# Issuing the stores of the residual rows from ScalarE's queue instead of SyncE's in a hybrid RG-LRU, attention and routed-experts layer

## The chip, the cores and the metric

The kernel runs on one core of a Trainium2 chip. The metric is the time of one execution on the device, in microseconds (us). The time of the kernel before is the median of three runs. The rows further down come from one more execution, taken by the hardware profiler. Engines are named as the profile names them: PE (TensorE, matmuls), PEld (its weight loads), DVE (VectorE), ACT (ScalarE), POOL (GpSimd), and SPq (the queue of SyncE, which here does nothing but issue DMAs).

## The reference, cut to what matters

One layer works on 512 rows of 1024 numbers, all in float32. A mixer (a gated linear recurrence and differential attention) gives `mix`. Then:

```
x1 = x + m2 * (mix @ w_out)                      # the residual rows; 512 x 1024
h2 = rmsnorm(x1, g2) * (1 + m4) + m3
aff = softmax(h2 @ w_router)                     # 16 experts
g, idx = top_k(aff.T, 64)                        # every expert takes its 64 best rows
y_e = (silu(h2[idx] @ w_gate[e]) * (h2[idx] @ w_up[e])) @ w_down[e]
out = x1;  out[idx] += m5 * g * y_e              # for all 16 experts
```

Each expert has three matrices of 1024 by 2816, so the 16 experts read 554 MB. That is most of the bytes that the kernel moves.

## The kernel before

**Stages.** The rows are worked on in four tiles of 128 rows, t = 0 to 3. After the mixer, `out_proj(t)` loads the tile of x into `X1[t]`, multiplies by `w_out` on PE in two halves of 512 columns, scales each half by `m2` on DVE (L1051), adds it into `X1[t]` (L1052), and takes its sum of squares on ACT (L1053, an `activation` with `Square`). When both halves are done, `X1[t]` is stored to `out` (L1054, the line that the change touches). Tiles 0 and 1 are done in `early_proj` while the second half of the attention still runs, tiles 2 and 3 in `late_proj`. `route(t)` (L1115) transposes `X1[t]` on PE, copies the transposes to SBUF (`h2T`), multiplies by the router's weights (`pl`), and makes the softmax (`lg`, `aux`). `largest` (L1143) finds the 64 largest values of each expert on DVE by eight rounds of MAX8 and MATCH_REPLACE8. The result is `least` (L1170), the threshold of each expert. From it follow the slots `slT`, the one-hot matrices `oh`, and with them `gather` (L1248), which makes an expert's 64 rows `xe` on PE. Then the expert loop begins: `up_rows` (L1278) multiplies `xe` by `w_gate` and `w_up`, in eight steps k of 128 rows; `down_part` does the rest, and adds the result into `out` in memory by an indirect DMA from POOL (L1319).

**The ring.** The weights of the experts go through a ring of 14 slots of 1408 KB. The order of the slots is: two of `ring0` (in the profile `ring<-`; for k = 0 of expert 0 they are loaded long before the stage looked at here), four of `R2` (`r<-`), four of `ring1` (`ring<-`), four of `R3` (`r<-`), and round again. A load into a slot waits until what used this memory before is done: the `ring1` slots hold parts of `w_out` until the last `out_proj` has read them, and the last two `R3` slots lie where the router's small tiles are until `least` is there. All of these loads are issued from SP's queue, and so are the four stores of `X1[t]`. A queue is worked off in order: a DMA that waits holds up those behind it.

**The order of the instructions.** Up to the expert loop, instructions aren't issued as written. The class `Flow` records them and lists them at each `flush` with a cost model of its own: `cost` (L206) gives the time for which an instruction holds its engine, the time to its result, and the bytes of a DMA; `schedule` (L290) takes again and again the instruction with the earliest start, on one engine the one with the higher level `lvl` where several are ready. The level is the length of the longest chain that hangs on an instruction, plus a random part (`SEEDS`). Copies and additions made by `copy` and `tt` may go to either of two engines, whichever is done earlier. An entry for SP is taken in the order of recording (`i`). The flushes are at L620, L1076 (it ends with `early_proj(0)` and `early_proj(1)`), L1172 (`late_proj`, `route`, `largest`) and L1328 (slots, the loads of expert 0, the first one-hot). In the profile everything recorded in this way stands under line L288. The tile framework merges the flushes, so that on SP loads of the last flush stand between stores of the flush before it.

Of the kernel before, what the change touches and what calls it, by code (L numbers as in the profile page):

```python
# [56 lines left out]
class Flow:  # L57
# [93 lines left out]
    def tt(self, o, a, b, op):  # L151

        self.add("vec", "tensor_tensor", (o, a, b), {"op": op}, [("gp", "tensor_tensor", (o, a, b), {"op": op})])
# [52 lines left out]
    def cost(self, e, m, a, k, out, r):  # L206

        n = 1
        for st, c in out.ap[1:]:
            n *= c  # L210
        nin = n
        if r:
            nin = 1
            for st, c in r[0].ap[1:]:
                nin *= c
        ps = any("PSUM" in str(v.tensor.space) for v in r + [out] if type(v.tensor).__name__ == "Tile")
        if e == "sp":
            return 0.06, 0.06, 4 * n * out.ap[0][1], None
        if e == "pe":
            f32r = "float32r" in str(r[0].dtype)  # L220
            if m == "transpose":
                c = 0.084 if f32r else 0.109
            elif f32r:
                c = max(n * (1 if n >= 256 else 4), 256) * 0.00046
            else:
                c = 2 * max(0.112, n * 0.00084) * (0.5 if out.ap[0][1] < 128 else 1.0)
            return c, c + 0.165, 0.0, None
        ptr = sum(1 for v in r[1:] if not [1 for st, c in v.ap[1:] if c > 1])
        if e == "act":
            fn = a[2].name if hasattr(a[2], "name") else str(a[2]).split(".")[-1]  # L230
            c = (nin / 1120.0 + 0.14 if ps else nin / 1215.0 + 0.205) + 0.08 * ptr
            acc = 0.18 if "accum_out" in k else 0.0
            return c + (acc if acc else -0.1), c + acc, 0.0, self.SETS.get(fn)
        if e == "vec":
            if m == "memset":
                c = n / 1000.0 + 0.06
            elif m in ("max", "match_replace"):
                c = max(n, nin) / 960.0 + 0.14
            elif m in ("tensor_copy", "tensor_scalar") and not ps:
                c = n / 1920.0 + 0.15  # L240
            elif m == "tensor_tensor_scan":
                c = n * 2.1 / 960.0 + 0.14
            else:
                c = nin / 960.0 + 0.15
            c += 0.06 * ptr
            return max(c - 0.085, 0.06), c, 0.0, None
        if m == "tensor_tensor" and k.get("op") == OP.pow:
            c = 0.38 + 0.175 * n
        else:
            c = {"tensor_tensor": 2.5, "memset": 0.9, "iota": 1.5, "tensor_scalar": 1.2, "tensor_copy": 1.2}.get(m, 3.5) * n / 1000.0 + 0.18  # L250
        return max(c - 0.035, 0.06), c, 0.0, None
# [38 lines left out]
    def schedule(self, ops):  # L290
# [10 lines left out]
        while len(order) < len(ops):  # L301
# [23 lines left out]
            for e2 in o["alt"]:  # L325
                ready[e2].remove(o)
            cost, lat = o["alt"][e][3:]
            if e == "pe":
                w = int(st / WINDOW)
                if st > 15 and work.get(w - 1, 0.0) < 0.6 * WINDOW:  # L330
                    cost, lat = 2 * cost, lat + cost
                work[w] = work.get(w, 0.0) + min(cost, (w + 1) * WINDOW - st)
                if st + cost > (w + 1) * WINDOW:
                    work[w + 1] = work.get(w + 1, 0.0) + st + cost - (w + 1) * WINDOW
# [28 lines left out]
def hybrid_block_kernel(ctx: ExitStack, tc: tile.TileContext, x, cx, w_ada, b_ada, w_in, w_out, w_router, w_gate,  # L363
# [3 lines left out]
    act, vec, gp, pe, sp = (flow.proxy(e) for e in ("act", "vec", "gp", "pe", "sp"))  # L367
# [62 lines left out]
    def raw():  # L430
        return X.tile([128, D], F32, name="raw", tag="raw", bufs=4)
# [70 lines left out]
    def mm3(o, lh, ll, rh, rl, first, last):  # L502
        pe.matmul(o, lh, rh, start=first, stop=False, skip_group_check=True)
        pe.matmul(o, lh, rl, start=False, stop=False, skip_group_check=True)
        pe.matmul(o, ll, rh, start=False, stop=last, skip_group_check=True)
# [46 lines left out]
    def rstd(o, ssum, n, w):  # L552
        gp.tensor_scalar(ssum, ssum, 1.0 / n, EPS, op0=OP.mult, op1=OP.add)
        gp.tensor_tensor(o, ssum, half[:, :w], op=OP.pow)
# [471 lines left out]
    X1 = [raw() for _ in range(4)]  # L1026
# [15 lines left out]
    def out_proj(t, mh, ml, m2row, bank, tmp):  # L1042
        ts = slice(t * 128, (t + 1) * 128)
        sp.dma_start(X1[t], x[ts, :])
        for q in range(2):
            c2 = slice(q * 512, (q + 1) * 512)
            po = bank()
            for k in range(KT):
                mm3(po, mh[k], ml[k], woH[k][:, c2], woL[k][:, c2], k == 0, k == KT - 1)
            tm = tmp()  # L1050
            vec.tensor_tensor(tm, po, m2row[:, c2], op=OP.mult)  # L1051
            tt(X1[t][:, c2], X1[t][:, c2], tm, OP.add)  # L1052
            act.activation(tm, X1[t][:, c2], AF.Square, accum_out=s2[:, t, q:q + 1])  # L1053
        sp.dma_start(out[ts, :], X1[t])  # L1054
        vec.tensor_tensor(s2[:, t, 2:3], s2[:, t, 0:1], s2[:, t, 1:2], op=OP.add)
        rstd(rs2[:, t:t + 1], s2[:, t, 2:3], D, 1)

    def early_proj(t):
        h6, l6 = (LR.tile([128, 6, 128], F32R, name=f"g{i}", tag=f"g{i}", bufs=2) for i in range(2))
        hl2 = LR.tile([128, 2, 2, 128], F32R, name="xc", tag="xc", bufs=2)  # L1060
        mh, ml = mix_parts(t, ((6, h6, l6), (2, hl2[:, 0], hl2[:, 1])))
        out_proj(t, mh, ml, m2e, ac, lambda: QK.tile([128, 512], F32, name="hl", tag="hl", bufs=2))
# [47 lines left out]
    def late_proj(t):  # L1110
        mh, ml = parts2 if t == 2 else mix_parts(t, ((KT, *(RT.tile([128, KT, 128], F32R, name=n) for n in ("mh", "ml"))),))
        out_proj(t, mh, ml, m2l, po_bank,
                 lambda: RT.tile([128, 512], F32, name="tm", tag="tm", bufs=2))
# [215 lines left out]
    act, vec, gp, pe, sp = nc.scalar, nc.vector, nc.gpsimd, nc.tensor, nc.sync  # L1329
# [77 lines left out]
```

## Time and profile before

| | us |
|---|---|
| median of three runs | 1722.05 (1720.24 to 1722.1) |
| the profiled execution: its time | 1720.25 |
| the profiled execution: span of the trace | 1718.4 |

| engine | busy us | share of the span |
|---|---|---|
| PE | 1466.9 | 85% |
| PEld | 800.5 | 47% |
| DVE | 406.3 | 24% |
| ACT | 317.4 | 18% |
| POOL | 164.7 | 10% |

The DMA engines moved 607.32 MB, 353 GB/s over the span. The stage with the stores lies between 354 us and 404 us of the span, the expert loop from 424 us on. A time of the span is 1.85 us short of the execution's own time, which is around it.

### The profile page before, as it was taken

Reading aid. Unit: us, or ns where it says so; the run is one execution under the profiler, and the core shown is the slowest. Engines: PE = TensorE matmul, PEld = TensorE weight load, DVE = VectorE, ACT = ScalarE, POOL = GpSimd, SP = SyncE. Lnnn points to the kernel's source line nnn. Section 1 sums busy time; section 2 is a strip of 40 time slices with the busy share of each in tenths; the row PEclk is TensorE's granted clock in tenths of the full one; section 3 lists DMA queues with packets and bytes.
Section 4 is the critical chain, followed back from the end, with each engine's and each line's share of the span. In section 5 each row is a group of like instructions: output and inputs, shape, how many; then the busy total and the mean of one; then the engine's idle time right before and its main releaser. Section 6 shows DMA issues by size and latency. Waiting matters only on the chain. (4 is left out here: it accounts for less than half of the span.)

```text
span 1718.4 us, 19014 instructions
## 1 busy us (share of the span) xinstructions
PE 1466.9 (85%) x8072; PEld 800.5 (47%) x8072; DVE 406.3 (24%) x786; ACT 317.4 (18%) x565; POOL 164.7 (10%) x160
## 2 busy tenths in 40 slices
PE   6988989897998997888788878887987798779877
PEld 3786788675445442433253334433432443244323
DVE  5889986835010010001010001000000000000101
ACT  5466765421101010101010001101010101010101
POOL 1194172300000000000000000000000000000000
PEclk9989999897989999899989998999999899989999
DMA  9535321356999999999999999999999999999996
GB/s 343 155 107 166 109 72 64 106 198 282 403 412 428 421 427 422 428 420 421 429 427 422 421 428 423 426 421 429 420 429 421 428 421 429 421 427 421 429 422 259
DMA packets 89375, 607.32 MB, mean 353 GB/s; under 512 B 12393, under 2 KB 31046, under 8 KB 40266
## 3 DMA queue, kind: packets, MB, share of 16 engines
q1 hardware_dynamic: 86986, 601.91, 84.9%
q0 software_dynamic: 2304, 4.20, 1.4%
q8 instruction: 63, 1.03, 0.2%
q14 instruction: 22, 0.18, 0.0%
HBM read 599.78 MB, written 6.29 MB: 353 GB/s over the span
## 5 line engine op out<-in xcount | busy, mean ns | idle before, releaser
L1283 PE MATMUL gu<-r,xe 128*64 128x512 f32 (+1 forms) x1752 | 386.2, 564 | 66.1 <-DMA r<-in_w_up_dram 65.7
L1283 PE MATMUL gu<-ring,xe 128*64 128x512 f32 (+1 forms) x1320 | 302.4, 574 | 54.0 <-DMA ring<-in_w_up_dram 54.0
L1283 PEld LDWEIGHTS gu<-r,xe 128*64 128x64 f32 x1752 | 148.3, 138 | 286.1 <-issue 190.5
L1283 PEld LDWEIGHTS gu<-ring,xe 128*64 128x64 f32 x1320 | 111.7, 140 | 227.2 <-issue 150.3
L1307 PE MATMUL y<-r,hT 128*64 128x512 f32 (+1 forms) x888 | 206.6, 604 | 0.0
L1307 PE MATMUL y<-ring,hT 128*64 128x512 f32 (+1 forms) x648 | 151.2, 597 | 0.0
L1319 POOL DMA_INDIRECT out_dram<-ys,ix x16 | 25.0, 1564 | 1283.3 <-DVE ys L1318 1283.3
L1292 DVE TENSOR_TENSOR sg<-sg,gu 64x512 f32<-64x512 f32 x96 | 58.1, 647 | 326.4 <-ACT sg L1291 326.1
L1307 PEld LDWEIGHTS y<-r,hT 128*64 128x64 f32 x888 | 76.9, 148 | 107.8 <-issue 96.5
L1291 ACT ACTIVATE sg<-gu 64x512 f32<-64x512 f32 x96 | 48.1, 552 | 425.0 <-PE gu L1283 424.8
L288 PE MATMUL ac<-w,ring 128*128 128x256 f32 x768 | 108.5, 298 | 10.1 <-DVE ring L288 4.9
L1318 DVE SCALAR_TENSOR_TENSOR ys<-y,gate,brow 128x512 f32<-128x512 f32 x16 | 12.0, 751 | 407.9 <-issue 382.7
L288 PEld LDWEIGHTS ac<-w,ring 128*128 128x128 f32 x768 | 101.3, 201 | 13.5 <-issue 4.4
L1254 ACT ACTIVATE xe<-y,B,A 128x128 f32<-128x128 f32 x32 | 14.6, 457 | 502.1 <-PE y L1252 502.1
L1298 PE MATMUL tr<-ident,sg 64*128 64x64 f32 x352 | 57.9, 319 | 53.5 <-DVE sg L1292 42.2
L1268 DVE COPY gate<-tr 128x1 f32<-128x1 f32 x16 | 2.5, 158 | 392.4 <-PE tr L1264 392.4
L1307 PEld LDWEIGHTS y<-ring,hT 128*64 128x64 f32 x648 | 56.3, 146 | 76.9 <-issue 68.9
L1298 PEld LDWEIGHTS tr<-ident,sg 64*128 64x128 f32 x352 | 50.5, 232 | 73.3 <-issue 45.2
L1299 ACT ACTIVATE hT<-tr 128x512 f32<-128x512 f32 (+1 forms) x48 | 26.9, 561 | 223.4 <-PE tr L1298 192.9
L288 PE MATMUL ac<-ring,w 128*128 128x512 f32 (+1 forms) x240 | 62.7, 388 | 1.5 <-POOL w L288 1.2
L288 PEld LDWEIGHTS ac<-ring,w 128*128 128x128 f32 x240 | 40.7, 191 | 9.2 <-POOL w L288 1.3
L288 ACT ACT_TABLE_LOAD x33 | 42.3, 1283 | 4.9 <-DVE lru L288 3.6
(254 smaller groups left out, 1269.9 us busy)
## 6 DMA issues: line engine op xcount, KB each, us to landing
r<-in_w_gate_dram SPq DMA_DIRECT2D x73, 1408.0 KB, 26.9
r<-in_w_up_dram SPq DMA_DIRECT2D x73, 1408.0 KB, 27.0
r<-in_w_down_dram SPq DMA_DIRECT2D x73, 1408.0 KB, 26.9
ring<-in_w_gate_dram SPq DMA_DIRECT2D x55, 1408.0 KB, 26.8
ring<-in_w_up_dram SPq DMA_DIRECT2D x55, 1408.0 KB, 26.8
ring<-in_w_down_dram SPq DMA_DIRECT2D x54, 1408.0 KB, 26.8
raw<-in_w_ada_dram SPq DMA_DIRECT2D x32, 512.0 KB, 3.8
raw<-in_w_in_dram SPq DMA_DIRECT2D x20, 512.0 KB, 4.6
```

What stands on the lines that cost most here:

```text
L288: getattr(self.eng[e], o["m"])(*o["a"], **o["k"])
L1254: act.activation(xe[:, k], pg, AF.Identity, bias=B2[:, k:k + 1], scale=A2[:, k:k + 1])
L1268: vec.tensor_copy(g_t, pi[:, 2 * pair + i:2 * pair + i + 1])
L1283: pe.matmul(b[hh * 64:(hh + 1) * 64, :n], xe[:, k, es], wgu[k][hh][:, f:f + n], start=(k == 0), stop=(k == KT - 1), skip_group_check=True)
L1291: act.activation(sg[64:128, f:f + n], b[:64, :n], AF.Silu)
L1292: vec.tensor_tensor(sg[64:128, f:f + n], sg[64:128, f:f + n], b[64:128, :n], op=OP.mult)
L1298: pe.transpose(pt[:, j - j0], cols[:, j], ident[64:128, 64:128])
L1299: act.activation(hT[:, j0:j1], pt[:, :j1 - j0], AF.Copy)
L1307: pe.matmul(y[hh * 64:(hh + 1) * 64, a % 512:a % 512 + b - a], hT[:, j], wd[a // FE][:, a % FE:a % FE + b - a], start=(j == 0), stop=(j == ...
L1318: vec.scalar_tensor_tensor(ys, y, g_t, m5row, op0=OP.mult, op1=OP.mult)
L1319: gp.indirect_dma_start(out=out.rearrange("t (h d) -> (t h) d", h=2), out_offset=bass.IndirectOffsetOnAxis(ap=ix[:, :1], axis=0), in_=ys, ...
```

## The change

The store of `X1[t]` at L1054 is issued from ScalarE's queue. Since `act` entries had no cost for a DMA in the planner, `cost` gets one: such an entry holds ACT for 0.4 us, its result is there after 4.0 us, and no bytes are booked. (For SP the planner books 0.06 us and the bytes.)

```diff
@@ cost @@
         ptr = sum(1 for v in r[1:] if not [1 for st, c in v.ap[1:] if c > 1])
+        if m == "dma_start":
+            return 0.4, 4.0, 0.0, None
         if e == "act":
@@ out_proj @@
             act.activation(tm, X1[t][:, c2], AF.Square, accum_out=s2[:, t, q:q + 1])
-        sp.dma_start(out[ts, :], X1[t])
+        act.dma_start(out[ts, :], X1[t])
         vec.tensor_tensor(s2[:, t, 2:3], s2[:, t, 0:1], s2[:, t, 1:2], op=OP.add)
```

## Rows read from the trace of the kernel before

**Rows 1.** Busy time by stretch: start and end, length, engines, PE clock, DMA share, GB/s.

```profile
core 0: us, PE busy (x) PEld busy (x) DVE busy (x) ACT busy (x) POOL busy (x), PEclk, DMA share, GB/s
427.00:430.00 3.00, 3.00 (x17) 1.05 (x14) 0.00 (x0) 0.00 (x0) 0.00 (x0) 1.00 0.00 0
...
440.00:460.00 20.00, 20.00 (x111) 8.68 (x108) 0.00 (x0) 1.37 (x3) 0.00 (x0) 1.00 1.00 422
...
520.00:1590.00 1070.00, 915.71 (x4758) 419.58 (x4754) 71.97 (x167) 86.28 (x173) 20.15 (x13) 0.95 1.01 424
```

**Rows 2.** Waits from 520 to 1590 us: total, times, longest.

```profile
PEld gu L1283 <- DMA r<-in_w_up_dram: 71.6, 36, 3.6
```

**Rows 3.** Timeline of SP's queue, 365 to 430 us: start, duration, what.

```profile
365.85 0.34 SPq L288 DMA_DIRECT2D out_dram<-raw  x1
...
368.10 0.42 SPq L288 DMA_DIRECT2D r<-in_w_gate_dram  x1
380.49 0.34 SPq L288 DMA_DIRECT2D out_dram<-raw  x1
380.88 0.43 SPq L288 DMA_DIRECT2D r<-in_w_up_dram  x1
...
403.18 0.34 SPq L288 DMA_DIRECT2D out_dram<-raw  x1
403.62 0.38 SPq L288 DMA_DIRECT2D ring<-in_w_gate_dram  x1
...
415.36 0.33 SPq L288 DMA_DIRECT2D r<-in_w_gate_dram  x1
...
429.89 0.33 SPq L288 DMA_DIRECT2D ring<-in_w_gate_dram  x1
```

**Rows 4.** Waits of SP's queue from 350 to 460 us.

```profile
SPq L288 <- DVE raw L288: 33.0, 3, 11.9
SPq L288 <- PE po L288: 13.0, 1, 13.0
```

**Rows 5.** Timeline of all engines, 367 to 430 us; in brackets idle before, releaser.

```profile
367.18 7.74 PE L288 MATMUL po<-ring,w 128*128 128x512 f32 x32 [0.61 <-ACT m2row L288]
...
402.49 0.67 DVE L288 TENSOR_TENSOR raw<-raw,tm 128x512 f32<-128x512 f32 x1
...
406.90 0.21 DVE L288 SCALAR_TENSOR_TENSOR lg<-pl,rs,brt 128x16 f32<-128x16 f32 x1
...
409.27 0.28 DVE L288 COPY vals<-pT 16x128 f32<-16x128 f32 x1
...
414.99 0.21 DVE L288 TENSOR_REDUCE least<-tops 16x1 f32<-16x65 f32 x1
...
424.16 5.70 PE L1283 MATMUL gu<-ring,xe 128*64 128x512 f32 x24
```

**Rows 6.** Timeline of ACT, 364 to 408 us.

```profile
364.58 0.63 ACT L288 ACTIVATE hl<-raw 128x512 f32<-128x512 f32 x1 [9.39 <-issue]
...
366.55 0.58 ACT L288 ACTIVATE m2row<-po 128x512 f32<-128x512 f32 x1
...
382.61 0.60 ACT L288 ACTIVATE h2T<-pt 128x512 f32<-128x512 f32 x1 [1.23 <-PE pl L288]
...
404.21 0.60 ACT L288 ACTIVATE h2T<-pt 128x512 f32<-128x512 f32 x1 [0.29 <-PE pt L288]
407.49 0.31 ACT L288 ACTIVATE aux<-lg,s 128x16 f32<-128x16 f32 x1 [2.68 <-DVE s L288]
```

**Rows 7.** The four stores: duration in ns, min/median/max.

```profile
L288 SPq DMA_DIRECT2D out_dram<-raw x4: 344/344/348, 354.4 to 403.2; - x4
```

**Rows 8.** DMA issues of the whole run: count, KB, median us to landing.

```profile
r<-in_w_gate_dram SPq DMA_DIRECT2D x73, 1408.0 KB, 26.9
```

**Rows 9.** Loads into R2 and R3, 366 to 420 us, to landing.

```profile
DMA to landing us min/median/max: 7.5/11.4/15.2
```

**Rows 10.** Timeline of DVE, the same kind of copy as ACT's h2T.

```profile
385.44 0.69 DVE L288 COPY h2T<-pt 128x512 f32<-128x512 f32 x1 [1.45 <-PE pl L288]
```

## The prediction

> **What bounds the kernel now.** I read the stretches first, to see which resource is full where; then the waits in the expert loop; then SP's own timeline and waits around the stores; last the timeline of all engines between the last store and the first expert, to see what lets the loop begin.
>
> From 520 to 1590 us the DMA engines are full: share 1.01 at 424 GB/s, while PE is busy for 915.71 of 1070 us [rows 1], and PE's weight loads wait for arriving weights (71.6 us on one of the kinds of load) [rows 2]. So the loop is bound by the stream of weights, and the end of the kernel is the time at which this stream becomes continuous, plus its bytes at 424 GB/s. A change ahead of the loop counts only if it moves that time.
>
> When does the stream become continuous? SP issues the load for the first ring slot that comes free again at 429.89 us [rows 3]. Ahead of it, from 427 to 430 us, the DMA engines are empty: share 0.00 [rows 1]. Everything that the 14 slots can hold has landed by 427 us, and nothing more may be asked for until PE is through with step k = 0 of expert 0, which runs from 424.16 us for 5.70 us, to 429.86 us [rows 5]. That release, and not an arrival, starts the stream. Right after it, from 440 to 460 us, PE is busy for 20.00 of 20 us [rows 1]: the slots in hand are enough, and it waits for no load.
>
> What sets 424.16 us is the router. The second half of `X1[3]` is added from 402.49 us; its logits come at 406.90, the transposed affinities at 409.27, `least` at 414.99, then the slots, the one-hots, the first gather [rows 5]. This chain contains no load and no store.
>
> **The change, part by part.** *Taken from SP.* Four issues of 0.344 us [rows 7], 1.4 us, and the time for which SP stood at them: three waits on `X1` (DVE raw), 33.0 us in total, the longest 11.9 us [rows 4]. Two of them hold ring loads. The store of tile 2 stands from 368.10 + 0.42 us to 380.49 us before a load into R2 that goes at 380.88; the store of tile 3 at 403.18 us stands before a load into `ring1` that goes at 403.62 [rows 3]. Without the stores, the first of these loads can go some 12 us earlier. The second can go earlier too, but not before the load ahead of it, which is held for 13.0 us by PE's last reading of `w_out` (PE po) [rows 4], so until 380.88 + 13.0 = 394 us: it gains less than 403.6 − 394 = 9.6 us. The load issued at 415.36 us [rows 3] waits for `least`, which ends at 414.99 + 0.21 = 415.20 us [rows 5]; it doesn't move by this.
>
> What is late next? Nothing that these loads feed. They land before 427 us already, and earlier landing lengthens the empty stretch before 429.89 us by as much. Gain at the end: 0 us, hidden by the router's chain. If that cover were gone, and the expert loop began as its weights came, the gain would be up to 9.6 us.
>
> The Trainium skill has a rule that speaks against such a change: in "DMA: Bandwidth & Descriptors", section "Issuing engines are not separate DMA queues", it says that DMAs started from several engines share the same 16 DMA engines, and that this "will only save the time on the sequencer". By that the saving would be 4 × 0.344 = 1.4 us of SP's time; the trace shows that SP is also freed of 33.0 us of waiting, which the rule doesn't speak of. By the rule or by the rows, the sum at the end stays 0.
>
> *Added to ACT.* The trace shows no DMA issued from ACT. From below its cost is nothing, if the issue runs beside ACT's datapath; a gain by the issue itself is excluded, since ACT has one more thing to do. From above, the nearest row is SP's issue of the same transfer, 0.344 us [rows 7]. In the planner the store has no instruction behind it, so its level is about 4 (14 with the boost of the early tiles), below the Square and below the copies, on which the router's chain hangs. It will stand behind the second Square of its tile, which waits for the same addition; the store then adds no wait of its own on `X1`. Behind it on ACT stand:
>
> Tile 0: the Squares of tile 1, before which ACT is idle for 9.39 us [rows 6]; hidden, cost 0. Tile 1: the copy of `m2row` at 366.55 us [rows 6], for which PE waits to begin the matmuls of tile 2 at 367.18 us [rows 5]; here 0 to 0.34 us are on the path. Tile 2: copies to `h2T` at 382.61 us after 1.23 us of idle time [rows 6]; hidden. Tile 3: the second `h2T` copy of the last tile at 404.21 us, after only 0.29 us of idle time, and it is in the router's chain: 0.344 − 0.29 = 0.05 us; or, if the copy goes first, the idle 2.68 us before 407.49 us take it [rows 6]: 0. If all this cover failed, four issues would cost 1.4 us. The sum on the path lies between 0 and 0.4 us. I take 0.3 us, near the upper end, because the only row for such an issue is SP's and the copy of `m2row` follows without a gap.
>
> *Moved in the planner.* The entry of 0.4 us shifts ACT's free time in its model, and the bytes of the four stores are no longer booked. Levels of other instructions keep their values: the store's own cost in the level was 4.02 (0.06 + 2.5 + 1.46 for its bytes) and is 4.0, and longer chains than the store's hang on the additions. So the order changes only where ACT's or SP's free time decides. The likeliest such change is a copy that goes to the other of its two engines. An `h2T` copy on DVE takes 0.69 us [rows 10] where ACT takes 0.60 [rows 6], and DVE is the fuller engine in the router's chain; one more there costs at most 0.7 us, one fewer gains as much. I take 0 and keep −0.7 to +2.8 us (four copies, two of tile 2 and two of tile 3) for the range.
>
> Sum against the profiled execution: 1720.25 + 0.3 = 1720.6 us. That execution lies 1.8 us (0.1%) below the median of the runs shown, so on the median I say 1722.05 + 0.3, about 1722.3 us.
>
> **The rivals.** *A: the freed loads shorten the kernel.* SP loses 33.0 us of waiting [rows 4], and the loop is bound by loads. If the stream's beginning depended on SP, the gain would be the smaller of the two advances that I could bound, up to 9.6 us: 1722.05 − 9.6 = 1712.5 us. For it: the full DMA engines from 520 us on. Against it: share 0.00 just before 429.89 us, with all slots filled [rows 1]. This rival is in the Trainium skill as well: "Perfetto Trace Analysis", section "DMA Optimizations", advises one issuing engine for inputs and another for outputs, for more dynamic spread. No row here shows the advice at work; the rows show where its gain would be lost. Chance 0.04.
>
> *B: ACT stands at a store for a DMA ahead of it.* In the stream a load of 1408 KB takes 1.44 MB / 424 GB/s = 3.4 us and lands 26.9 us after its issue [rows 8, 1], so eight are under way; I read that as a limit of eight, with the next DMA held until the eighth before it has landed. If that limit counts over both queues, the store of tile 3 could find the loads that now run ahead of it unlanded. Loads of this stage take up to 15.2 us to land [rows 9]; one issued at 403.62 us would free ACT at 418.8 us, and the copy at 404.21 would come 14.6 us late: 1722.05 + 14.6 = 1736.7 us. It decides from the point at which eight ring loads stand between that store and the store of tile 2. Against it: between them there can be only one load into R2, four into `ring1` and two into R3, seven, because the next ones wait for `least`; the eighth back is then a DMA of about 380 us, long landed. Chance 0.05.
>
> *C: the planner's order changes for the worse* by more than copies: a matmul block of a late tile put behind a route, or a larger part of the router's chain behind `largest`. The rows bound it only loosely; four copies and the issue come to 2.8 + 0.4 = 3.2 us, 1725.3 us, and more than that needs a second misfortune. Chance 0.05 of more than 3.4 us slower; 0.02 that the new order gains as much.
>
> *D: the change doesn't do what it says*, because the loads freed on SP wait for memory anyway. Then the profile differs only by the stores' queue, and the time is the forecast's.
>
> **How the numbers follow.** A measurement of this kernel can tell about 0.2%, 3.4 us. The forecast, D included, has 0.84 and lies within that. Faster: A 0.04 and C 0.02, 0.06. Slower: B 0.05 and C 0.05, 0.10. The range takes the forecast's own bounds, which hold more than 8 in 10: the lowest run less one copy, 1720.24 − 0.7 = 1719.5 us; the highest run with four copies and the issue, 1722.1 + 2.8 + 0.4 = 1725.3 us.
>
> **What would show it.** In the profile after: stores under ACT's queue; the R2 load now at 380.88 us issued near 369; a `ring1` load issued between 394 and 403 us; the DMA engines empty for longer before the load that follows step k = 0; and that load within 1 us of 429.89. The forecast is wrong if that load moves by more than 3.4 us, or if ACT shows idle time before an `h2T` copy that a DMA ends.

## The result, and the profile after

| | before | after |
|---|---|---|
| median, us | 1721.42 (4 runs, 1720.24 to 1722.1) | 1740.22 (4 runs, 1738.95 to 1742.37) |
| span of the profiled execution, us | 1718.4 | 1739.5 |

The kernel became slower: ratio 1.0112 (95% interval 1.0100 to 1.0124), about 19 us. The forecast was no change.

SP's timeline of the kernel after (start, duration, what) answers to [rows 3]:

```profile
369.76 0.47 SPq L290 DMA_DIRECT2D r<-in_w_up_dram  x1
404.25 0.33 SPq L290 DMA_DIRECT2D r<-in_w_gate_dram  x1
...
418.99 0.33 SPq L290 DMA_DIRECT2D r<-in_w_gate_dram  x1
...
433.91 0.33 SPq L290 DMA_DIRECT2D ring<-in_w_gate_dram  x1
...
439.87 6.77 SPq L290 DMA_DIRECT2D r<-in_w_down_dram  x4
446.69 0.44 SPq L290 DMA_DIRECT2D ring<-in_w_gate_dram  x1
447.18 0.43 SPq L290 DMA_DIRECT2D ring<-in_w_up_dram  x1
447.66 0.44 SPq L290 DMA_DIRECT2D ring<-in_w_gate_dram  x1
448.15 0.47 SPq L290 DMA_DIRECT2D ring<-in_w_up_dram  x1
470.65 7.18 SPq L290 DMA_DIRECT2D ring<-in_w_down_dram  x4
```

The stores are gone, and the last load into `R2` goes at 369.76 instead of 380.88 us. But the four loads into `ring1` (k = 3 and 4 of expert 0), which before went from 394 to 404 us, now go from 446.69 us. They stand behind four loads of `w_down` into `R2`, and those wait for PE to be through with steps k = 1 and 2. Before, the same `w_down` loads came behind all of expert 0's other loads, as two more rows of SP's timeline before show:

```profile
394.11 0.33 SPq L288 DMA_DIRECT2D ring<-in_w_gate_dram  x1
...
435.85 6.77 SPq L288 DMA_DIRECT2D r<-in_w_down_dram  x4
```

A queue is worked off in order, so four slots stayed empty for 44 to 53 us longer than before.

PE's timeline of the kernel after (in brackets the idle time before, and what ended it):

```profile
445.74 1.16 PE L1254 MATMUL y<-oh,raw 128*128 128x128 f32 x8
461.30 1.94 PE L1285 MATMUL gu<-ring,xe 128*64 128x512 f32 x2 [14.40 <-DMA ring<-in_w_gate_dram]
464.53 6.50 PE L1285 MATMUL gu<-ring,xe 128*64 128x512 f32 x22 [1.29 <-DMA ring<-in_w_up_dram]
```

PE is ready for step k = 3 at 446.9 us and stands 14.40 + 1.29 = 15.7 us for weights. Busy time by stretch of the kernel after (the first, second and last row answer to [rows 1]; those between show PE's stand and the stretch behind it):

```profile
core 0: us, PE busy (x) PEld busy (x) DVE busy (x) ACT busy (x) POOL busy (x), PEclk, DMA share, GB/s
...
430.00:434.00 4.00, 4.00 (x21) 1.31 (x18) 0.00 (x0) 0.00 (x0) 0.00 (x0) 0.98 0.00 0
...
440.00:460.00 20.00, 6.90 (x40) 3.35 (x39) 0.00 (x0) 0.92 (x2) 0.00 (x0) 0.77 1.00 412
...
452.00:460.00 8.00, 0.00 (x0) 0.00 (x0) 0.00 (x0) 0.00 (x0) 0.00 (x0) 0.50 1.01 429
...
468.00:472.00 4.00, 4.00 (x24) 1.81 (x19) 0.00 (x0) 0.00 (x0) 0.00 (x0) 1.00 0.66 228
...
460.00:520.00 60.00, 52.28 (x276) 22.47 (x278) 4.04 (x10) 7.23 (x13) 0.00 (x0) 0.88 0.95 391
...
520.00:1590.00 1070.00, 922.78 (x4770) 422.53 (x4768) 74.67 (x176) 86.35 (x173) 21.93 (x14) 0.94 1.01 424
```

The stream is as fast as before (424 GB/s). It still becomes continuous at the load behind k = 0, now at 433.91 us, with the DMA engines empty ahead of it. What differs is how much had landed by then: 10 slots instead of 14, as these two rows of the 66 us ahead of that load show, first of the kernel before, then of the kernel after:

```profile
363.89:429.89 66.00, 53.17 (x271) 41.00 (x269) 34.70 (x131) 12.70 (x32) 2.71 (x9) 0.82 0.74 295
```

```profile
367.91:433.91 66.00, 53.07 (x256) 41.76 (x255) 33.19 (x128) 9.93 (x26) 3.04 (x10) 0.77 0.52 199
```

(295 − 199) GB/s × 66 us = 6.3 MB less; four loads are 5.77 MB, which take 13.6 us at 424 GB/s. (The rest is a load of x, 0.5 MB, which falls into the first of the two windows only.)

ACT is innocent. Its timeline in the kernel after, around two of the stores (answers to [rows 6]):

```profile
367.10 0.63 ACT L290 ACTIVATE hl<-raw 128x512 f32<-128x512 f32 x1 [0.61 <-DVE raw L290]
367.15 0.34 ACTq L290 DMA_DIRECT2D out_dram<-raw  x1
...
367.73 0.58 ACT L290 ACTIVATE m2row<-po 128x512 f32<-128x512 f32 x1
...
406.55 0.63 ACT L290 ACTIVATE tm<-raw 128x512 f32<-128x512 f32 x1 [0.45 <-DVE raw L290]
406.56 0.34 ACTq L290 DMA_DIRECT2D out_dram<-raw  x1
```

These two stores, and that of tile 2 at 382.17 us, are issued inside a Square, and the copy of `m2row` follows its Square without a gap. The store of tile 0 goes at 355.68 us, between the two Squares of its tile, and there too ACT has no idle time behind it.

**Where the order comes from.** The section on the kernel says that SP's entries are taken in the order of recording. This holds only among those that can start at once. Two lines of `schedule`, as they stand for SP (the terms for the other engines are left out at `...`):

```
st = rt[i] if rt[i] > f else f        # f: SP's clock; rt: when the slot is free
key = (st if st > f + 0.05 else f, i if e == "sp" else ...)
```

An entry whose slot comes free later than SP's clock is sorted by that time. This is the kernel's own list at its last flush, in the list's own times (a model's, not the chip's):

```
loads of expert 0      before (SP clock 366.66)    after (SP clock 312.14)
R2     k = 1, 2        366.66 to 366.84            312.14 to 312.32
ring1  k = 3, 4        366.90 to 367.08            357.49 to 362.73
R3     k = 5, 6        behind ring1                312.38 to 312.56
ring0  k = 7           367.38                      312.62 to 312.68
R2     w_down          374.66 to 386.68            320.14 to 332.15
ring1  w_down          behind R2's                 from 376.21
```

The store of tile 3 had put SP's clock at 366.66, later than the last release of a `ring1` slot that the list knows (358.19 to 363.6). All loads could then start at once, and recording order held. Without the stores SP's clock is 312.14. The `ring1` loads are then late, and are sorted behind every load whose release the list doesn't know. For `R3` it doesn't know the router's tiles, and for `ring0` and the second round of `R2` not PE's steps. It puts that second round, the `w_down` loads, 4.0 us apart at 320 to 332, where on the chip they wait until 439.87 us.

### The profile page after: what moved, and what is told of

It reads as the page before. It is cut to its first block, busy times and chain, and to the rows that moved or that the text cites. A ratio compares the mean times of both kernels' runs of the same rounds, so it can differ in the third digit from the quotient of the medians.

```text
span 1739.5 us, 19002 instructions
## 1 busy us (share of the span) xinstructions
PE 1477.2 (85%) x8072; PEld 805.0 (46%) x8072; DVE 408.5 (23%) x787; ACT 316.1 (18%) x563; POOL 165.4 (10%) x161
## 5 line engine op out<-in xcount | busy, mean ns | idle before, releaser
L1285 PE MATMUL gu<-r,xe 128*64 128x512 f32 (+1 forms) x1752 | 390.4, 570 | 64.9 <-DMA r<-in_w_up_dram 64.7
L1256 ACT ACTIVATE xe<-y,B,A 128x128 f32<-128x128 f32 x32 | 14.6, 458 | 496.1 <-PE y L1254 496.1
```

The lines of the kernel that those rows point to most:

```text
L1256: act.activation(xe[:, k], pg, AF.Identity, bias=B2[:, k:k + 1], scale=A2[:, k:k + 1])
L1285: pe.matmul(b[hh * 64:(hh + 1) * 64, :n], xe[:, k, es], wgu[k][hh][:, f:f + n], start=(k == 0), stop=(k == KT - 1), skip_group_check=True)
```

## Experiments

Theory 1 (the order): the kernel is slower because the list, without the stores on SP, puts the `ring1` loads behind the `w_down` loads. The rivals: the store on ACT's queue costs the time, or the changed order of the router's instructions on PE, DVE and ACT does. Once it is the loads' order, two readings are left: the bytes that haven't landed when the stream becomes continuous (1a), or PE's standing at the late loads (1b).

Each time stands beside that of the kernel before in the same comparison.

**1. List as before, stores issued from ACT.** An edit of the kernel before: the planner books the store on SP, only the instruction is issued from ACT.

```diff
-                getattr(self.eng[e], o["m"])(*o["a"], **o["k"])
+                getattr(self.eng[o.get("issue", e)], o["m"])(*o["a"], **o["k"])
...
         sp.dma_start(out[ts, :], X1[t])
+        flow.ops[-1]["issue"] = "act"
```

> The stores are entered in the planner as SP's, as in the kernel before, and only when the instructions are issued do they go to ScalarE's queue. Every other instruction keeps the order of the kernel before. Theory 1 (the loss lies in the order of the ring's loads that the planner makes once the stores are gone from SP's list, and in later copies of the router): no change against before, 1721.4 us within 2 us, and the first ring load after step k = 0 issued within 1 us of 429.9 us. Theory 2 (the loss lies in the queue: ScalarE's own issues, or two queues on the same DMA engines): about 1740 us, like the changed kernel.

Measured: 1721.55 us (11 runs, 1720.0 to 1724.51) beside 1721.37 us (29 runs); ratio 1.0001 (0.9992 to 1.0011). SP's timeline:

```profile
368.43 0.52 SPq L288 DMA_DIRECT2D r<-in_w_up_dram  x1
395.84 0.33 SPq L288 DMA_DIRECT2D ring<-in_w_gate_dram  x1
...
400.50 0.33 SPq L288 DMA_DIRECT2D ring<-in_w_gate_dram  x1
...
430.43 0.33 SPq L288 DMA_DIRECT2D ring<-in_w_gate_dram  x1
```

Here the loads moved as the prediction wanted (368.43, and 400.50 for 403.62), and it was worth nothing: the load behind k = 0 still goes at 430.43 us. So the issue from ACT costs nothing that can be measured, and rival A is wrong too.

**2. List as after, stores issued from SP.** The opposite edit of the kernel after: the same line in `flush`, and

```diff
         act.dma_start(out[ts, :], X1[t])
+        flow.ops[-1]["issue"] = "sp"
```

> The stores are planned as ScalarE's, as in the changed kernel, and issued on SP's queue; every other instruction keeps the order of the changed kernel. Theory 1 (order of the ring's loads): about 1740 us, within 2 us of the changed kernel, with the four ring1 loads of expert 0 again behind the first w_down loads, at about 447 us. Theory 2 (the queue): back to about 1722 us.

Measured: 1740.96 us (4 runs, 1739.13 to 1742.86); ratio 1.0117 (1.0098 to 1.0135). SP's timeline:

```profile
437.49 6.76 SPq L290 DMA_DIRECT2D r<-in_w_down_dram  x4
444.30 0.42 SPq L290 DMA_DIRECT2D ring<-in_w_gate_dram  x1
```

The stores are back on SP, and the whole loss stays. It is the list and not the queue.

**3. The kernel after, with expert 0's loads kept in the order of recording.** `flow.chain` makes each recorded load follow the one before it; all other engines keep the order of the kernel after.

```diff
+    flow.chain = True
     wgu, wd = load_gu(0), load_dn(0)
+    flow.chain = False
```

> The changed kernel, with the loads of expert 0 held in the order in which they are recorded; all else is in the order of the changed kernel. Theory 1: the four ring1 loads are again in memory before step k = 0 ends, so the 4 x 3.4 = 13.6 us of transfers that the changed kernel puts off, and some 3 us of gaps behind them, come back; what stays is that the router ends about 4 us later than before: 1725 us, between 1723 and 1727 us. Theory 2 (the queue): about 1740 us still.

Measured: 1721.21 us (12 runs, 1719.12 to 1724.21); ratio 1.0000 (0.9991 to 1.0009). All of it comes back. SP's timeline:

```profile
399.87 0.33 SPq L290 DMA_DIRECT2D ring<-in_w_gate_dram  x1
...
431.41 0.33 SPq L290 DMA_DIRECT2D ring<-in_w_gate_dram  x1
```

I had left some 4 us for the router's order, since the load behind k = 0 went at 433.91 instead of 429.89 us in the kernel after. This was wrong: with the same router order the time is that of the kernel before, to within 0.0009 × 1721 = 1.6 us. Of those 4.02 us, 1.35 were there already at the load at 334.36 us (before: 333.01), ahead of all that the change touches.

**4. Bytes alone: k = 6's pair behind k = 7's.** An edit of the kernel before. Two loads that would go at 415 us go behind the release by k = 0 instead, early enough that PE should not stand.

```diff
     def load_gu(e):
-        return [pre if e + k == 0 else [load_ex(e, k, i) for i in range(2)] for k in range(KT)]
+        if e:
+            return [[load_ex(e, k, i) for i in range(2)] for k in range(KT)]
+        res = [pre] + [[load_ex(e, k, i) for i in range(2)] for k in range(1, 6)]
+        held = [slot(), slot()]
+        last = [load_ex(e, 7, i) for i in range(2)]
+        for i in range(2):
+            sp.dma_start(held[i], (w_gate, w_up)[i][e, 768:896, :])
+        return res + [held, last]
```

> The kernel before, stores on SP, with one pair of loads issued later: those for step k = 6 of expert 0 stand behind those for k = 7, which wait for step k = 0. They should still land some 10 us before PE needs them, so PE gets no new wait in expert 0. Theory 1a (what counts is how many bytes of weights have landed when the stream becomes continuous): two loads of 3.4 us each are put off, 1721.4 + 6.8 = 1728 us. Theory 1b (what counts is PE's stall inside expert 0, 15.7 us in the changed kernel): no change, 1721.4 us within 2 us.

Measured: 1726.38 us (10 runs, 1724.28 to 1728.56); ratio 1.0029 (1.0019 to 1.0039), 3.3 to 6.7 us. SP's timeline, and then all of PE's waits from 424 to 520 us (total, times, longest), none of which is for a load:

```profile
429.18 0.33 SPq L288 DMA_DIRECT2D ring<-in_w_gate_dram  x1
...
430.08 0.37 SPq L288 DMA_DIRECT2D r<-in_w_gate_dram  x1
```

```profile
PE tr L1305 <- DVE sg L1299: 4.0, 1, 4.0
PE tr L1305 <- ACT hT L1306: 0.7, 1, 0.7
PE tr L1271 <- DVE ix L1276: 0.5, 1, 0.5
```

So 1a holds by itself: a load that is put off costs time without any engine waiting for that load. Two loads are 2 × 3.4 = 6.8 us of stream that the empty stretch ahead of the release no longer takes; that lies at the upper edge of what the times allow. The time is lost later, at other loads: from 520 to 1590 us PE's waits for loads are 107.2 us, and 100.3 us in the kernel before.

**5. SP's clock set back.** One line in the kernel before, with the stores left on SP:

```diff
+    flow.free["sp"] = 0.0
     wgu, wd = load_gu(0), load_dn(0)
```

> The kernel before, stores on SP's queue and planned there, except that the planner's clock of SP is set back to 0 ahead of the list for expert 0. All engines but SP keep the order of the kernel before. Theory 1 (what the stores did was to hold SP's clock in the planner late, so that all loads counted as ready and stayed in the order of recording): the four ring1 loads go behind the first w_down loads as in the changed kernel, and the time is that of the changed kernel, less up to 2 us for the router's order: 1738 to 1741 us. The rival (the changed order of the router's copies and multiplications is a good part of the loss): clearly less than the changed kernel, under 1735 us.

Measured: 1732.5 us (4 runs, 1731.54 to 1735.67) beside 1720.67; ratio 1.0075 (1.0052 to 1.0098), less than expected, and under the 1735 us that the rival named. But the run doesn't decide between them, for it made another order than I had meant. SP's timeline:

```profile
428.34 0.33 SPq L288 DMA_DIRECT2D ring<-in_w_gate_dram  x1
...
429.19 0.42 SPq L288 DMA_DIRECT2D ring<-in_w_gate_dram  x1
...
430.98 0.48 SPq L288 DMA_DIRECT2D ring<-in_w_up_dram  x1
434.30 6.77 SPq L288 DMA_DIRECT2D r<-in_w_down_dram  x4
```

The `ring1` loads went behind k = 7's pair, but ahead of the `w_down` loads, since I had set back SP's clock and not the planner's clock of the transfers. So SP's clock alone does reorder loads, which is part of theory 1, but the run is no copy of the kernel after. It is useful as another size: four loads put off, and PE standing only 2.1 us.

**6. k = 4's pair alone behind the `w_down` loads.** Kernel before, loads chained as in 3; `load_gu` leaves k = 4's pair out, and `load_dn` issues it:

```diff
...
+            elif (e, k) == (0, 4):
+                res.append([slot(), slot()])
...
+            if (e, i) == (0, 4):
+                for j in range(2):
+                    sp.dma_start(wgu[4][j], (w_gate, w_up)[j][0, 512:640, :])
```

> The kernel before, with one pair of loads put off, as in the experiment with step k = 6, but so far that PE must stand for them: those of step k = 4 of expert 0 stand behind the first four w_down loads. From the issue times before, PE should wait 8 to 11 us inside expert 0. If only the bytes put off count (two loads), the time is that of the experiment with k = 6, 5 us over before, within 2 us: 1724.5 to 1728.5 us. If PE's standing adds a part of its own, because the slots that it reads come free later, it lies above: 1729 us and more.

Measured: 1735.24 us (4 runs, 1733.27 to 1737.34) beside 1720.67; ratio 1.0084 (1.0060 to 1.0107). Two loads cost 14.6 us here and 5.0 us in 4, so bytes are not all, and 1b has a part. PE stands 8.2 + 1.3 = 9.5 us (its timeline), and soon after the DMA engines run dry (busy time by stretch):

```profile
459.69 1.94 PE L1294 MATMUL gu<-ring,xe 128*64 128x512 f32 x2 [8.16 <-DMA ring<-in_w_gate_dram]
462.93 7.82 PE L1294 MATMUL gu<-ring,xe 128*64 128x512 f32 x22 [1.30 <-DMA ring<-in_w_up_dram]
```

```profile
468.00:472.00 4.00, 4.00 (x22) 1.96 (x20) 0.00 (x0) 0.12 (x1) 0.00 (x0) 0.90 0.38 99
...
460.00:520.00 60.00, 53.57 (x273) 22.66 (x273) 4.78 (x11) 6.78 (x12) 0.79 (x1) 0.87 0.92 374
```

While PE stands it frees no slot; once everything asked for has landed, there is a gap in the stream until PE has used up a slot again.

**7. The exact order of the kernel after, everything else as before.** As 6, with `e == 0 and k in (3, 4)`, so that both pairs go behind the first four `w_down` loads.

> The kernel before, its stores on SP and all engines but SP in its order, with the loads of expert 0 forced into exactly the order that they have in the changed kernel: the two ring1 pairs (k = 3 and k = 4) behind the first four w_down loads. Theory 1 (that order is the whole loss): about 1739 us, 1737 to 1741 us. From the first ring load after step k = 0 to the last DVE ys of the kernel it should take 17.7 us more than before, and PE should stand 14 to 16 us for a ring1 load. The rival (a part of the loss, up to 4 us, comes from the order of the router in the changed kernel): 1735 us or less.

Measured: 1737.91 us (4 runs, 1734.85 to 1742.74) beside 1721.55; ratio 1.0104 (1.0082 to 1.0126). SP's timeline and PE's waits from 424 to 500 us:

```profile
434.67 6.77 SPq L288 DMA_DIRECT2D r<-in_w_down_dram  x4
441.49 0.45 SPq L288 DMA_DIRECT2D ring<-in_w_gate_dram  x1
```

```profile
PE gu L1295 <- DMA ring<-in_w_gate_dram: 14.2, 1, 14.2
...
PE gu L1295 <- DMA ring<-in_w_up_dram: 1.3, 1, 1.3
```

With this order alone the kernel before has the loss of the kernel after: the interval of the result (1.0100 to 1.0124) lies inside this one.

**The sum over all kernels.** From the load behind k = 0 to the last addition of the expert loop (DVE `ys`), in each profiled execution. The `ys` of the kernel before, and of the kernel after:

```profile
1710.97 0.75 DVE L1318 SCALAR_TENSOR_TENSOR ys<-y,gate,brow 128x512 f32<-128x512 f32 x1 [25.01 <-issue]
```

```profile
1732.28 0.75 DVE L1320 SCALAR_TENSOR_TENSOR ys<-y,gate,brow 128x512 f32<-128x512 f32 x1 [25.22 <-issue]
```

"Bytes" are 3.4 us for each load put off; "gaps" are 60 us × (1.01 − DMA share from 460 to 520 us), 1.01 being the share before.

| kernel | load behind k = 0 | last `ys` | between | against before | put off | PE stands | bytes | gaps |
|---|---|---|---|---|---|---|---|---|
| before | 429.89 | 1710.97 | 1281.08 | | 0 | 0 | 0 | 0 (1.01) |
| 1 | 430.43 | 1710.66 | 1280.23 | −0.9 | 0 | 0 | 0 | 0 (1.01) |
| 2 | 431.53 | 1729.76 | 1298.23 | +17.2 | 4 | 15.5 | 13.6 | 3.6 (0.95) |
| 3 | 431.41 | 1712.16 | 1280.75 | −0.3 | 0 | 0 | 0 | 0 (1.01) |
| 4 | 429.18 | 1716.20 | 1287.02 | +5.9 | 2 | 0 | 6.8 | 0 (1.01) |
| 5 | 428.34 | 1722.16 | 1293.82 | +12.7 | 4 | 2.1 | 13.6 | 0 (1.01) |
| 6 | 432.59 | 1726.59 | 1294.00 | +12.9 | 2 | 9.5 | 6.8 | 5.4 (0.92) |
| 7 | 428.71 | 1726.77 | 1298.06 | +17.0 | 4 | 15.5 | 13.6 | 3.0 (0.96) |
| after | 433.91 | 1732.28 | 1298.37 | +17.3 | 4 | 15.7 | 13.6 | 3.6 (0.95) |

Bytes and gaps together come within 0.9 us of each difference. That is as near as single executions go: runs 1 and 3, with no load put off, differ from before by −0.9 and −0.3 us, and a share with two decimals leaves 0.3 us. (The 17.7 us in the expectation of run 7 end at the last `ys` but one; at the last it is 17.3 us.) PE's standing does not add up as such (15.7 us of it go with 3.6 us of gaps): the stream runs on while PE stands, and only the part in which no slot is free is lost.

No version beat the kernel before; 1 and 3 equal it.

## Why the prediction was wrong

**What held.** The loop is bound by the stream; it becomes continuous (but for the gaps above) at the load behind k = 0, with nothing moving just ahead of it. Loads that are issued earlier are worth nothing (run 1), so rival A is out. A store on ACT costs nothing that can be measured (0.3 us forecast; run 1: −1.4 to +1.9 us). The Trainium skill says in "DMA: Bandwidth & Descriptors", section "Issuing engines are not separate DMA queues", that issuing from several engines saves only sequencer time; run 1's ratio of 1.0001 agrees, in that nothing more was saved. Rival B is out: from 340 to 430 us no wait of ACT is ended by a DMA. So is D: the loads freed on SP did move. The `R2` load went at 369.76 us, as forecast.

**The step that failed** is "Moved in the planner": "the order changes only where ACT's or SP's free time decides. The likeliest such change is a copy that goes to the other of its two engines." The first sentence was right, and I followed only half of it. I worked out ACT's free time, and did not ask what SP's free time decides: the order of SP's own loads. The stores were the last entries that held SP's clock at the time of the router, and with them went the order in which all of expert 0's loads are issued. I had also read the rule for SP as plain order of recording, as the section on the kernel has it; the key's first part is the start.

From this follows the false sentence of "Taken from SP": "The second can go earlier too". It went 44 us later (447.66 us). And "Everything that the 14 slots can hold has landed by 427 us" and "the slots in hand are enough" were read from the kernel before and carried over without a question; in the kernel after only 10 slots are filled, and PE stands 15.7 us. The term "Moved in the planner" stood at 0 us, with −0.7 to +2.8 us for the range; the order of the loads alone costs 16.4 us (run 7, between medians).

A second step failed with it: "A change ahead of the loop counts only if it moves that time", the time at which the stream becomes continuous. In run 7 the load behind k = 0 goes at 428.71 us, 1.18 us earlier than before, and the kernel is 16.4 us slower. The end is that time plus the bytes that are still to come, and the prediction took these bytes as fixed. For the same reason its sign, that this load moves by more than 3.4 us, is none: it was met in the kernel after (4.02 us), but in run 7 the loss comes without it. The sign that would have told is the other one, a `ring1` load between 394 and 403 us, which did not come.

**The rivals.** C had the right class, the planner's order, but on the wrong engines (matmul blocks and the router's chain) and at a chance of 0.05. The copies that I expected did change engine: the second `h2T` copy of the last tile goes to DVE, for one. Run 3 bounds all of that at 1.6 us.

**The size.** Between the medians the kernel became 18.8 us slower. The span of the profiled execution grew by 21.1 us: +17.3 in the stream, +4.0 by the later load behind k = 0, −0.2 behind the last `ys`. The 17.3 are shown (run 7: +17.0 with the order alone). The 4.0 of this one execution are not pinned on the change: between profiled executions of the kernels this load lies between 428.34 and 433.91 us, and run 3 returns to the time of before with the same router order. What stays open is whether the router's order costs something below 1.6 us, and the up to 0.9 us that the sum leaves.

## What to carry to other kernels

When an instruction leaves an engine whose order a list scheduler makes, ask what that instruction's time was holding in place: here a late store made every load "ready", and so kept the written order, which was the right one. A queue that is worked off in order needs its order from real releases; where the model doesn't know some of them, write the order down (run 3's two lines). And in a kernel bound by a stream, count the bytes that have landed by the time at which the stream becomes continuous: here each load put off past it cost about its full transfer, even where no engine waited for that load, while a consumer that stood cost only the gap that its late slots made.

## What the hardware showed beside this

A DMA issued from ACT lies in time inside a running `ACTIVATE`: the store at 367.15 to 367.49 us inside the Square from 367.10 to 367.73 us. The four issues took 338 to 374 ns, about as on SP (344 to 348). The DMA engines kept their share of 1.01 (429 GB/s) while PE did nothing from 452 to 460 us; so the stream needs PE for the slots, not at every moment. PE's granted clock in that stretch was 0.50, which is 1.2 GHz: the first matmuls after the stand are slow (two in 1.94 us, 22 in 6.50 us, where the same step of 24 took 4.94 us in the kernel before). Whether that costs anything no run shows: the DMA engines run partly dry from 468 to 472 us (share 0.66), and the next load, into a slot that waits for this step, goes at 470.65 us.
